# Second attention four heads at a time, another issue order of the last expert weights, and operands at one place modulo 256 bytes

## The chip, the core and the metric

The kernel runs on one core of one Trainium2 chip. The metric is the device time in microseconds; of the kernel before three runs were timed, with a median of 1975.59 us (1973.17 to 1978.7).

## The reference

Two transformer blocks follow each other on 512 tokens of 1024 features, all in float32. What matters of them here:

```python
# block 1
n = rms_norm(h, g_mix); q, k, v, u, bg, cg, ga, gc = split(n @ w_in + b_in)
m = sigmoid(ga) * (chunked_rel_attention(q, k, v) @ w_pa) + sigmoid(gc) * (short_conv(u, bg, cg) @ w_pc)
h = h + m @ w_o
h = h + hier_moe(rms_norm(h, g_ffn))     # 32 experts of width 512, the 2 best of one group for each token
h = h + sigmoid(rms_norm(h, g_ple) @ w_ple_gate + b_ple_gate) * (p @ w_ple_proj)
# block 2: hs = 16 meta tokens and h, 528 rows
for layer in range(2):
    x = rms_norm(hs, norm_mix_pre[layer])
    mix = pool_mixer(x) if layer == 0 else sliding_window_attention(x, k_blk, v_blk)
    hs = hs + rms_norm(mix, norm_mix_post[layer])
    x = rms_norm(hs, norm_ffn_pre[layer])                   # swiglu of width 2816
    hs = hs + rms_norm((silu(x @ w_gate) * (x @ w_up)) @ w_down, norm_ffn_post[layer])
    if layer == 0: k, v = rms_norm(hs, kv_norm) @ w_k + b_k, ... @ w_v + b_v      # 2 heads of 64
# sliding_window_attention: 16 heads of 64, a block of 128 queries sees 128 keys before it and its own 128
logits = q k^T / 8 + bias;  m = max(logits, sink);  p = exp(logits - m);  out = (p / (sum p + exp(sink - m))) v
```

## The kernel before, in words

Block 1 is written out by hand in class `Net`; block 2 is class `Rest`, where generators for "sides" (norms, attention heads, combination) are stepped between the matmuls of a main line, by a planner's clock. In block 2 all instructions are issued through one helper, so that in the profile nearly all of them carry line 1195.

*Matmuls in three terms.* Weights come by DMA as fp32 (`raw`), ScalarE rounds them to fp32r (`whi`) and VectorE takes the rest (`wlo`). A product is `hi*hi + hi*lo + lo*hi` (`mm3`, lines 226 and 1431): three matmuls on TensorE of 128 rows by 256 to 512 columns. The activations are split in the same way: `nT`, `mT`, `pT` in block 1, `x` (normed features, two tiles of 8 x 528) and `act` (four chunks of 528 in each of two tiles, by `act4`, line 1485) in block 2. Layer 0 works on 528 rows, as halves of 256 and 272 columns, layer 1 on 512.

*The second attention* (layer 1) is a side, `heads(t, hq, d)` (line 2018): one block of 128 queries, and of four neighbouring heads the two of one parity `d`. Heads of parity `d` have their queries and keys in partitions 64d to 64d + 63. So the two score matmuls of a call (fp32, 64 rows deep, 256 keys, 144 in the first block, into one PSUM bank) use one half of the array's rows. Maximum and bias on VectorE, exponential on ScalarE and division on VectorE follow, then four transposes into `tmp`, one or two copies to `pt`, two value matmuls (`acc<-pt,v`, 128 rows, two heads side by side as 256 columns, into partitions 0 to 63 of a bank), and `cut` into `oT`. 32 calls are made, in the order of `self.quads` (run, line 2141), up to four in flight: `room("s", 4)` waits for a score buffer. Beside them the main line works on `q`, `kv` and `o_proj`. fp32 matmuls leave two records in the trace, fp32r ones and transposes one.

*The experts* (`moe`, line 834) take weights in half units of 1 MB from a ring of places: `todo` lists them in the order in which they are used, `ring` gives each its place, `load()` issues DMAs on SyncE's queue as long as the next place is free, and a `Take` frees a place once the matmuls on it are issued. `PLACES` is the cycle of 16, `LAST_PLACES` the last eight. `embed_load` (line 621), called two experts before the end, asks for `p`, `w_ple_proj` and `h`; before the last expert `embed_weight` and `embed_turn` split and transpose these, and `embed` (line 648) computes `p @ w_ple_proj` after it. `Rest.run` then starts: `combine` reads the experts' results `y2` back, `bands` and `col` load constants.

*Places.* A tile's place in a partition is the sum of the tiles ahead of it in its pool. By these sums the weights, `wide` and `nT` begin at 64 modulo 256 bytes, `mT` and `pT` at 96, `act` at 224, and rows of 528 fp32 (2112 bytes) move by 64 bytes modulo 256 with every row.

Of the kernel before, what the change touches and what calls it, by code (L numbers as in the profile page):

```python
# [20 lines left out]
P = 128  # L21
D = 1024
S = 512
# [18 lines left out]
LAST_PLACES = ("wide",) * 4 + ("wide2",) * 2 + ("wide",) * 2  # L42
# [91 lines left out]
class Net:  # L134
# [35 lines left out]
    def tmp(self, name="tmp"):  # L170
        self.n_ += 1
        return self.ps.tile([P, 512], F32, tag="tmp", bufs=2, name=f"{name}{self.n_}")

# [91 lines left out]
    def mixer(self):  # L265
# [98 lines left out]
        for t, ps in enumerate(vs):  # L364
            nc.vector.tensor_tensor(vt[:, t], ps, bb[:, 2], OP.add)

# [184 lines left out]
    def head(self):  # L551
# [18 lines left out]
        self.wrt = self.rt.tile([P, KC, 36], F32, name="wr")  # L570
        nc.sync.dma_start(self.wrt[:, :, 0:4], a["w_group"].rearrange("(p kc) n -> p kc n", kc=KC))
# [262 lines left out]
    def moe(self):  # L834
# [145 lines left out]
        with tc.manual_schedule():  # L980
            for e in range(TURN, N_E):
# [252 lines left out]

class Stream:
# [120 lines left out]
class Rest:  # L1356
# [5 lines left out]
    def __init__(self, net, out):  # L1362
# [8 lines left out]
        self.st = Stream(net, self.nc, self.clock)  # L1371
        self.halves = [slice(0, 256), slice(256, L2)]
# [112 lines left out]
    def act4(self):  # L1485

        return [x.rearrange("p (a b) -> p a b", a=4) for x in self.act()]
# [8 lines left out]
    def gain(self, src):  # L1496
        g, was = self.tile("gain", 3, [P, D]), self.clock.cur
        self.nc.sync.dma_start(g, bcast(src, P))
        self.clock.cur = was
        return g  # L1500

    def col(self, src, name):

        g, was = self.one([P, KC], name), self.clock.cur
        self.nc.sync.dma_start(g, src.rearrange("(c p) -> p c", p=P), allow_slow_non_contiguous=True)
# [176 lines left out]
    def pool_weights(self):  # L1682

        a = self.a
        g = self.col(a["norm_mix_pre"][0], "gpool")
# [119 lines left out]
    def up_out(self, pss, A, cs, n, key):  # L1805
# [10 lines left out]
        yield from self.cut(A[0][:, cs], A[1][:, cs], sl)  # L1816
# [201 lines left out]
    def heads(self, t, hq, d):  # L2018
# [6 lines left out]
        hs = slice(4 * hq + d, 4 * hq + 4, 2)  # L2025
# [3 lines left out]
        yield from self.room("s", 4)  # L2029
        place = self.claim("s", 4).append  # L2030
        s = self.scores[self.n_heads % 4]
        self.n_heads += 1
        st = self.net.small.tile([P, 4, 2], F32, tag="st", name="st")
        yield from self.room("acc", 6)
        ps, end = self.acc()
        pv = ps.rearrange("p (a b) -> p a b", a=2)[:, :, :n]
        q, c0, b0 = self.qT[t // 2], P * (t % 2), 64 * d
        e = N_META + (t + 1) * P
        for i in range(2):
            nc.tensor.matmul(pv[:, i], q[b0:b0 + 64, 2 * hq + i, c0:c0 + P], self.kT[g][b0:b0 + 64, e - n:e],  # L2040
                             start=True, stop=True)
        self.mark(("s", t, hq, d))
        yield
        for i in range(2):
            V.tensor_tensor_reduce(s[:, i, :n], pv[:, i], self.bias[hq][:, 2 * i + d, m0:], 1.0, NEG, OP.add, OP.max,
                                   st[:, 0, i:i + 1])
        end(True)
        V.tensor_tensor(st[:, 0], st[:, 0], self.snk[:, hs], OP.max)
        V.tensor_scalar(st[:, 1], st[:, 0], -1.0, None, op0=OP.mult)
        V.tensor_tensor(st[:, 3], self.snk[:, hs], st[:, 0], OP.subtract)  # L2050
        yield
        for i in range(2):
            nc.scalar.activation(s[:, i, :n], s[:, i, :n], AF.Exp, bias=st[:, 1, i:i + 1],
                                 accum_out=st[:, 2, i:i + 1])
# [4 lines left out]
        for i in range(2):  # L2059
            V.tensor_scalar(s[:, i, :n], s[:, i, :n], st[:, 2, i:i + 1], None, op0=OP.mult)  # L2060
        yield
        yield from self.room("pt", 2)
        turn = self.claim("pt", 2).append
        PT = self.tile("pt", 2, [P, 512])
        yield from self.room("tmp", 2)
        ps, end = self.tmp()
        for c, a, b in ((0, 0, k0), (256, k0, n)):
            for i in range(2):
                nc.tensor.transpose(ps[:b - a, c + i * P:c + i * P + P], s[:, i, a:b], self.net.ident)
# [3 lines left out]
        if k0 < P:  # L2073
            nc.scalar.copy(PT[:k0, :256], ps[:k0, :256])
            nc.scalar.copy(PT[:, 256:], ps[:, 256:])
        else:
            nc.scalar.copy(PT, ps)
        end(True)
        yield
        yield from self.room("acc", 6)  # L2080
        ps, end = self.acc()
        vp = self.vt[NT] if t == 0 else self.vt[t - 1]
        gs = slice(64 * g, 64 * g + 64)
        po = ps[0:64, :256]
# [251 lines left out]
```

## Time and profile before

| | before |
|---|---|
| median of 3 runs | 1975.59 us |
| the profiled execution | 1978.86 us |
| its span, first to last instruction | 1977.0 us |
| PE busy | 1928.8 us (98%) |
| DVE busy | 831.9 us (42%) |
| ACT busy | 671.9 us (34%) |
| mean granted clock of PE | 0.986 |

PE is TensorE's matmul queue, PEld its weight loads, DVE VectorE, ACT ScalarE, POOL GpSimd, SP SyncE, which issues the DMAs. Busy time is the union of an engine's instructions; the end of a matmul is modelled, so a busy PE need not be at its peak. `acc<-kt,y 64*128 64x256` is a matmul into tile `acc` with `kt` streamed and `y` stationary: 64 rows by 128 columns of the array, 256 columns streamed. In a timeline neighbours of one kind stand in one row with their count.

### The profile page before, as it was taken

The numbers are of one execution on the slowest core, as the hardware profiler recorded it, in microseconds if no ns is written. First come the engines' busy times: TensorE is split into PE (matmuls) and PEld (weight loads), VectorE is DVE, ScalarE is ACT, GpSimd is POOL, SyncE is SP. The second block draws the span as 40 slices with busy tenths as digits, with TensorE's granted clock in tenths as the row PEclk, the third lists the DMA queues.
The fourth block names the chain that finished last, engine by engine and source line by source line (L and its number), as shares of the span: only waits on it lengthen the run. The fifth ranks groups of instructions, "written<-read, shape, count | busy, mean of one in ns | idle before, by whom it ended". The sixth has DMA issues, their size and how long they took to land. (4 is left out here: it accounts for less than half of the span.)

```text
span 1977.0 us, 27975 instructions
## 1 busy us (share of the span) xinstructions
PE 1928.8 (98%) x11330; PEld 1488.8 (75%) x11330; DVE 831.9 (42%) x1836; ACT 671.9 (34%) x1434; POOL 108.6 (5%) x183
## 2 busy tenths in 40 slices
PE   9999999999999999979999999999999999999998
PEld 7766888754554544527899999999987698888886
DVE  5477343511111111117574333334887874233334
ACT  4333332221111111125463333223876663233232
POOL 2100000010000000001111000000100000000000
PEclk9999999999999999988899999999999999999999
DMA  6222326689999999986035223224432244223322
GB/s 193 79 86 64 106 79 255 229 325 417 417 418 417 418 418 418 405 316 211 2 119 191 86 86 98 74 86 128 140 96 86 86 155 154 85 96 101 102 75 75
DMA packets 182102, 365.59 MB, mean 185 GB/s; under 512 B 25909, under 2 KB 127925, under 8 KB 162514
## 3 DMA queue, kind: packets, MB, share of 16 engines
q1 hardware_dynamic: 178834, 357.47, 49.3%
q0 software_dynamic: 2560, 4.20, 0.6%
q8 instruction: 90, 1.47, 0.3%
q10 hardware_dynamic: 576, 2.10, 0.3%
q14 instruction: 42, 0.34, 0.1%
HBM read 355.34 MB, written 12.58 MB: 186 GB/s over the span
## 5 line engine op out<-in xcount | busy, mean ns | idle before, releaser
L1195 PE MATMUL acc<-x,whi 128*128 128x256 f32 (+2 forms) x2560 | 547.4, 310 | 2.0 <-DVE x L1195 2.0
L1195 PEld LDWEIGHTS acc<-x,whi 128*128 128x128 f32 x2560 | 416.3, 189 | 32.4 <-issue 4.1
L1195 PE MATMUL acc<-x,wlo 128*128 128x256 f32 (+2 forms) x1280 | 395.7, 309 | 0.0
L1195 DVE TENSOR_TENSOR wlo<-raw,whi 128x512 fp32r<-128x512 f32 (+1 forms) x348 | 225.0, 689 | 317.9 <-ACT whi L1195 316.7
L1195 ACT ACTIVATE whi<-raw 128x512 fp32r<-128x512 f32 (+1 forms) x348 | 196.9, 617 | 338.4 <-PE acc L1195 278.9
L1195 PEld LDWEIGHTS acc<-x,wlo 128*128 128x128 f32 x1280 | 241.8, 189 | 12.5 <-DVE wlo L1195 0.2
L104 DVE TENSOR_TENSOR hd<-acc,sl 64x512 f32<-64x512 f32 x32 | 33.9, 1060 | 334.5 <-ACT sl L101 334.5
L1195 PE MATMUL acc<-whi,act 128*128 128x512 f32 x480 | 156.9, 398 | 0.0
L71 PEld LDWEIGHTS tmp<-one,n 128*128 128x128 f32 x1024 | 116.7, 192 | 25.2 <-issue 25.1
L1195 PE MATMUL acc<-act,whi 128*128 128x256 f32 (+1 forms) x704 | 130.5, 286 | 0.6 <-ACT act L1195 0.5
L96 PE MATMUL acc<-wide,xT 128*64 128x512 f32 x544 | 125.2, 603 | 0.0
L71 PE MATMUL tmp<-one,n 128*128 128x128 f32 x1024 | 122.5, 278 | 1.5 <-DVE one L61 1.5
L228 PE MATMUL acc<-wide,whi 128*128 128x512 f32 x288 | 115.5, 401 | 0.0
L230 PE MATMUL acc<-wide,wlo 128*128 128x512 f32 x288 | 112.5, 390 | 0.0
L229 PE MATMUL acc<-wide,whi 128*128 128x512 f32 x288 | 112.2, 390 | 0.0
L1195 PEld LDWEIGHTS acc<-act,whi 128*128 128x128 f32 x704 | 109.3, 188 | 1.1 <-ACT act L1195 0.7
L224 DVE TENSOR_TENSOR wlo<-raw,whi 128x1024 fp32r<-128x1024 f32 x56 | 68.1, 1222 | 96.4 <-ACT whi L221 96.2
L1195 PEld LDWEIGHTS acc<-whi,act 128*128 128x128 f32 x480 | 90.1, 188 | 24.3 <-issue 2.5
L1195 PE MATMUL acc<-act,wlo 128*128 128x256 f32 (+1 forms) x352 | 100.1, 284 | 0.0
L125 ACT COPY ys<-acc 128x512 f32<-128x512 f32 x32 | 18.8, 587 | 224.4 <-PE acc L119 224.4
L1195 PE MATMUL acc<-wlo,act 128*128 128x512 f32 x240 | 95.0, 396 | 0.0
L96 PEld LDWEIGHTS acc<-wide,xT 128*64 128x64 f32 x544 | 37.4, 138 | 67.5 <-issue 66.0
(449 smaller groups left out, 2671.8 us busy)
## 6 DMA issues: line engine op xcount, KB each, us to landing
wide<-in_w_dram SPq DMA_DIRECT2D x92, 1024.0 KB, 15.7
ew<-in_w_dram SPq DMA_DIRECT2D x60, 1024.0 KB, 19.9
raw<-in_w_gate_up_dram SPq DMA_DIRECT2D x52, 1024.0 KB, 5.1
raw<-in_w_in_dram SPq DMA_DIRECT2D x20, 1024.0 KB, 5.2
raw<-in_w_down_dram SPq DMA_DIRECT2D x18, 1024.0 KB, 5.2
raw<-in_w_o_dram SPq DMA_DIRECT2D x12, 1024.0 KB, 5.9
raw<-in_w_q_dram SPq DMA_DIRECT2D x8, 1024.0 KB, 7.0
raw<-in_w_down_dram SPq DMA_DIRECT2D x8, 768.0 KB, 4.5
```

Source lines behind the costliest of these rows:

```text
L71: self.nc.tensor.matmul(self.ps[:, k % 4], self.net.n2[t][:, k * P:(k + 1) * P], self.one[:, t].rearrange("p j s -> p (j s)"), start=t == ...
L96: self.nc.tensor.matmul(self.ps[SL * i:SL * i + SL], x, w(r), start=kc == 0, stop=kc == KC - 1)
L104: self.nc.vector.tensor_tensor(self.hd[SL:].rearrange("q fc p -> q p fc"), v(self.ps[SL:]), v(sl[SL:]), OP.mult)
L125: self.nc.scalar.copy(self.ys, self.py)
L224: self.nc.vector.tensor_tensor(lo, x, hi.bitcast(F32), OP.subtract)
L228: mm(out, l[0], r[0], start=start, stop=False)
L229: mm(out, l[0], r[1], start=False, stop=False)
L230: mm(out, l[1], r[0], start=False, stop=stop)
L1195: r = f(*a, **k)
```

## The change

- *Heads.* `heads(t, hq)` now handles four heads. Its four score matmuls go to two banks, alternating: `d = 0` in the upper and `d = 1` in the lower 64 rows of the array. Bias, maximum, exponential and division stay as many instructions per head; the small operations on `st` cover four heads. Each half of the keys has its own transposes (four into one `tmp`), one copy of 128 x 512 to a `pt` tile, and two value matmuls, where `d` chooses partitions 0 to 63 or 64 to 127 of one bank. One `cut` of all 128 partitions writes `oT`. Two calls are in flight at most; a call needs both `pt` buffers.
- *Last expert weights.* `LAST_PLACES` names two `wide2`, two `y` and four `wide`. `embed_turn` and `embed_weight` come after the last expert.
- *Small loads.* The six columns of gains and bias (`cols`) are loaded in the first block's mixer; `bands` and `combine` change places.
- *Places.* Unused tiles named `even` and the move of `lt` shift `mT` and `pT` by 32 bytes. `Halves` keeps a half of 256 columns in rows of 256 fp32, and the other half behind them: `x` in layer 0 (offset 48 fp32) and in layer 1's first steps up to `o_proj`, and `act` in layer 0. From `o_proj` on layer 1 has `x`, `act` and `oT` in rows of 512. `meta` and `vt` share a tile.

```diff
-LAST_PLACES = ("wide",) * 4 + ("wide2",) * 2 + ("wide",) * 2
+LAST_PLACES = ("wide2",) * 2 + ("y",) * 2 + ("wide",) * 4
...
+        self.cols = {nm: self.col(src, nm) for nm, src in (
+            ("gpool", a["norm_mix_pre"][0]), ("gf0", a["norm_ffn_pre"][0]), ("gkv", a["kv_norm"]),
+            ("gq", a["norm_mix_pre"][1]), ("gf1", a["norm_ffn_pre"][1]), ("bq", a["b_q"]))}
+        self.const.tile([P, 16], F32, name="even")
...
+        self.rt.tile([P, 56], F32, name="even")
...
-        lt = self.lt = self.small.tile([36, P], F32, tag="lt", bufs=1, name="lt")
+        lt = self.lt = self.rt.tile([36, P], F32, tag="lt", bufs=1, name="lt")
...
-                if e == N_E - 1:
-                    self.wproj = [self.embed_weight(hf) for hf in range(2)]
-                    self.embed_turn()
                 expert(e)
+            self.embed_turn()
+            self.wproj = [self.embed_weight(hf) for hf in range(2)]
...
+class Halves:
+
+
+    def __init__(self, t, rows, at=0):
+
+        n = rows * 256
+        self.parts = [x.rearrange("p (a b) -> p a b", a=rows) for x in (t[:, at:at + n], t[:, n:])]
+        self.parts[1] = self.parts[1][:, :, at:at + L2 - 256]
+
+    def __getitem__(self, at):
+        p, k, cs = at
+        c0 = cs.start or 0
+        x = self.parts[c0 >= 256]
+        if c0 >= 256:
+            cs = slice(c0 - 256, cs.stop - 256)
+        assert cs.stop <= x.shape[2]
+        return x[p, k, cs]
+
+
+class Row:
+
+
+    def __init__(self, x, k):
+        self.x, self.k = x, k
+
+    def __getitem__(self, at):
+        return self.x[at[0], self.k, at[1]]
...
-    def room(self, tag, bufs):
+    def room(self, tag, bufs, n=1):
 
         ring = self.rings.setdefault(tag, deque())
-        while len(ring) == bufs and not ring[0]:
+        while not all(list(ring)[:max(0, len(ring) + n - bufs)]):
...
-    def act4(self):
-
-        return [x.rearrange("p (a b) -> p a b", a=4) for x in self.act()]
+    def act4(self, halves=False):
+
+        if halves:
+            return [Halves(x, 4) for x in self.act()]
+        return [x[:, :4 * S].rearrange("p (a b) -> p a b", a=4) for x in self.act()]
...
-                new = self.act4()
+                new = self.act4(halves=not self.wide)
                 for k in range(4):
-                    act[f + k] = [x[:, k] for x in new]
+                    act[f + k] = [Row(x, k) for x in new]
...
-        self.vt = [self.one([P, P], f"v{t}") for t in range(NT + 1)]
-        self.bq = self.col(a["b_q"], "bq")
...
-    def heads(self, t, hq, d):
+    def heads(self, t, hq):
         nc, V = self.nc, self.V
         m0 = P - N_META if t == 0 else 0
         n = 256 - m0
         k0 = n - P
         g = hq // 2
+        snk = self.snk[:, 4 * hq:4 * hq + 4].rearrange("p (i d) -> p d i", d=2)
         yield ("q", t // 2, hq)
         yield ("v", t)
         yield ("v", t - 1 if t else NT)
+        yield from self.room("s", 2)
+        place = self.claim("s", 2).append
+        s = self.scores[self.n_heads % 2]
         self.n_heads += 1
+        st = self.net.small.tile([P, 4, 2, 2], F32, tag="st", name="st", bufs=2)
+        yield from self.room("acc", 6, 2)
+        banks = [self.acc() for _ in range(2)]
+        pv = [ps.rearrange("p (a b) -> p a b", a=2)[:, :, :n] for ps, _ in banks]
+        q, c0 = self.qT[t // 2], P * (t % 2)
+        e = N_META + (t + 1) * P
+        for i in range(2):
+            for d in range(2):
+                b = slice(64 * d, 64 * d + 64)
+                nc.tensor.matmul(pv[d][:, i], q[b, 2 * hq + i, c0:c0 + P], self.kT[g][b, e - n:e], start=True, stop=True)
+        self.mark(("s", t, hq))
+        yield
+        for d in range(2):
+            for i in range(2):
+                V.tensor_tensor_reduce(s[:, d, i, :n], pv[d][:, i], self.bias[hq][:, 2 * i + d, m0:], 1.0, NEG,
+                                       OP.add, OP.max, st[:, 0, d, i:i + 1])
+            banks[d][1](True)
+        V.tensor_tensor(st[:, 0], st[:, 0], snk, OP.max)
+        V.tensor_scalar(st[:, 1], st[:, 0], -1.0, None, op0=OP.mult)
+        V.tensor_tensor(st[:, 3], snk, st[:, 0], OP.subtract)
+        yield
+        for d in range(2):
+            for i in range(2):
+                nc.scalar.activation(s[:, d, i, :n], s[:, d, i, :n], AF.Exp, bias=st[:, 1, d, i:i + 1],
+                                     accum_out=st[:, 2, d, i:i + 1])
+        nc.scalar.activation(st[:, 3], st[:, 3], AF.Exp)
+        yield
+        V.tensor_tensor(st[:, 2], st[:, 2], st[:, 3], OP.add)
+        V.reciprocal(st[:, 2], st[:, 2])
+        for d in range(2):
+            for i in range(2):
+                V.tensor_scalar(s[:, d, i, :n], s[:, d, i, :n], st[:, 2, d, i:i + 1], None, op0=OP.mult)
+        yield
+        PT = []
+        for a, b in ((0, k0), (k0, n)):
+            yield from self.room("pt", 2)
+            turn = self.claim("pt", 2).append
+            x = self.tile("pt", 2, [P, 512])
+            yield from self.room("tmp", 2)
+            ps, end = self.tmp()
+            for d in range(2):
+                for i in range(2):
+                    c = (2 * d + i) * P
+                    nc.tensor.transpose(ps[:b - a, c:c + P], s[:, d, i, a:b], self.net.ident)
+            yield
+            nc.scalar.copy(x[:b - a], ps[:b - a])
+            end(True)
+            PT.append((x[:b - a], turn))
+        place(True)
+        self.next_heads()
+        yield
         yield from self.room("acc", 6)
         ps, end = self.acc()
+        gs = slice(64 * g, 64 * g + 64)
+        v = [(self.vt[NT] if t == 0 else self.vt[t - 1])[:k0, gs], self.vt[t][:, gs]]
+        for j in range(2):
+            for d in range(2):
+                nc.tensor.matmul(ps[64 * d:64 * d + 64, :256], v[j], PT[j][0][:, 256 * d:256 * d + 256],
+                                 start=j == 0, stop=j == 1)
+            PT[j][1](True)
+        yield
+        c = 2 * (hq % 2)
+        o = [x[:, c:c + 2, t * P:(t + 1) * P] for x in self.oT[hq // 2]]
+        yield from self.cut(*o, ps[:, :256].rearrange("p (a b) -> p a b", a=2))
         end(True)
+        self.mark(("a", t, hq))
...
-                self.until(*[("a", t, i, d) for i in range(4) for d in range(2)])
+                self.until(*[("a", t, i) for i in range(4)])
                 if mix is None:
-                    self.until(*[("s", t, i, d) for t in ts for i in range(4) for d in range(2)])
+                    self.until(*[("s", t, i) for t in ts for i in range(4)])
...
-        self.x = [self.one([P, KC, L2], f"x{i}", F32R) for i in range(2)]
-        meta = self.one([N_META, D], "meta")
+        xs = [self.one([P, KC * (256 + 320)], f"x{i}", F32R) for i in range(2)]
+        self.x, self.wide = [Halves(x, KC, 48) for x in xs], False
+        meta = self.tile("meta", 1, [P, D])[:N_META]
...
+        self.side(self.combine(y2))
+        self.step_side()
         self.bands()
         self.rg = self.one([P, NT], "rg")
-        self.side(self.combine(y2))
-        self.step_side()
         self.bg = self.gain(a["b_ple_gate"])
         self.side(self.pool_weights(), 4.0)
         nc.sync.dma_start(meta, a["meta"])
-        self.gkv, self.gq = self.col(a["kv_norm"], "gkvc"), self.col(a["norm_mix_pre"][1], "gqc")
-        self.gf0, self.gf1 = [self.col(a["norm_ffn_pre"][i], f"gf{i}") for i in range(2)]
...
-        self.scores = [x[:, i] for x in [self.big().rearrange("p (a k b) -> p a k b", a=2, k=2) for _ in range(2)]
-                       for i in range(2)]
+        self.scores = [self.big().rearrange("p (a k b) -> p a k b", a=2, k=2) for _ in range(2)]
         self.n_heads = 0
-        self.quads = deque((t, hq, d) for t in (3, 2, 0, 1) for hq in range(4) for d in range(2))
+        self.quads = deque((t, hq) for t in (3, 2, 0, 1) for hq in range(4))
...
+        vt = self.tile("meta", 1, [P, D])
+        self.vt = [vt[:, P * t:P * t + P] for t in range(NT + 1)]
...
-        for _ in range(4):
+        for _ in range(2):
...
+        self.x, self.wide = [x[:, :KC * S].rearrange("p (a b) -> p a b", a=KC) for x in xs], True
...
```

## Rows read from the trace of the kernel before

**Rows 1.** the page: span; busy us (share), instructions of each engine

```profile
span 1977.0 us, 27975 instructions
...
PE 1928.8 (98%) x11330; PEld 1488.8 (75%) x11330; DVE 831.9 (42%) x1836; ACT 671.9 (34%) x1434; POOL 108.6 (5%) x183
```

**Rows 2.** windows, attention: us; busy (x) PE PEld DVE ACT POOL; PEclk, DMA, GB/s

```profile
1425.00:1577.00 152.00, 151.74 (x912) 112.67 (x911) 125.31 (x504) 107.69 (x336) 2.20 (x4) 1.00 0.28 92
```

**Rows 3.** PE timeline, attention: start us, us, operation, shapes, records

```profile
1487.98 0.28 PE L1195 MATMUL acc<-x,wlo 128*128 128x256 f32 x1
1488.19 1.13 PE L1195 MATMUL acc<-kt,y 64*128 64x256 f32 x4
1489.25 1.08 PE L1195 MATMUL acc<-pt,v 128*64 128x256 f32 x4
1490.26 0.51 PE L1195 MATMUL acc<-x,whi 128*128 128x256 f32 x2
1490.60 0.28 PE L1195 MATMUL acc<-x,wlo 128*128 128x256 f32 x1
...
1493.81 0.77 PE L1195 MATMUL acc<-kt,y 64*128 64x144 f32 x8
...
1532.88 1.22 PE L1195 MATMUL acc<-pt,v 16*64 16x256 f32 x4
...
1555.86 1.14 PE L1195 MATMUL acc<-kt,y 64*128 64x256 f32 x8
1556.99 2.09 PE L1195 MATMUL acc<-pt,v 128*64 128x256 f32 x8
```

**Rows 4.** PE timeline, end of experts; in brackets idle time before and releaser

```profile
853.63 3.60 PE L119 MATMUL acc<-wide,hT 128*64 128x512 f32 x16
860.56 1.06 PE L644 MATMUL acc<-ident,n 128*128 128x128 f32 x8 [3.33 <-DMA n<-in_p_dram]
...
868.66 0.46 PE L110 MATMUL acc<-ident,hd 64*128 64x64 f32 x4 [1.76 <-DVE hd L104]
876.62 6.57 PE L119 MATMUL acc<-wide,hT 128*64 128x512 f32 x16 [7.49 <-DMA wide<-in_w_dram]
...
883.11 0.50 PE L228 MATMUL acc<-pwhi,pT 128*128 128x512 f32 x1
...
894.41 0.60 PE L1195 MATMUL tmp<-ident,h 128*128 128x128 f32 x4
```

**Rows 5.** SyncE's queue, end of the experts: start us, us, transfer, count

```profile
817.36 28.52 SPq L874 DMA_DIRECT2D wide<-in_w_dram  x12
...
861.83 4.00 SPq L874 DMA_DIRECT2D wide<-in_w_dram  x2
...
886.53 2.18 SPq L1195 DMA_DIRECT2D act<-y  x4
```

**Rows 6.** windows, before the last expert loads

```profile
834.00:844.00 10.00, 10.00 (x64) 5.53 (x65) 1.49 (x2) 0.59 (x1) 0.00 (x0) 1.00 0.69 256
```

**Rows 7.** windows of 3-term matmuls (512, 512, 256 columns); PE timeline, `mT` stationary

```profile
200.00:360.00 160.00, 160.00 (x704) 131.74 (x703) 60.47 (x70) 46.14 (x54) 1.33 (x6) 1.00 0.43 150
1650.00:1960.00 310.00, 310.00 (x1339) 251.03 (x1338) 109.14 (x171) 93.02 (x168) 0.93 (x1) 1.00 0.28 92
1615.40:1646.20 30.80, 30.80 (x262) 30.70 (x261) 16.85 (x36) 14.30 (x33) 0.00 (x0) 1.00 0.64 210
...
362.94 0.40 PE L228 MATMUL acc<-whi,mT 128*128 128x512 f32 x1
...
367.14 0.40 PE L228 MATMUL acc<-whi,mT 128*128 128x512 f32 x1
```

**Rows 8.** groups by form, attention: count, busy us, mean ns, idle before

```profile
L1195 PE MATMUL acc<-pt,v 128*64 128x256 f32 x112 | 29.9, 391 | 0.1
...
L1195 PE MATMUL acc<-kt,y 64*128 64x256 f32 x96 | 20.1, 401 | 0.1
...
L1195 DVE TENSOR_TENSOR act<-acc,act 64x256 fp32r<-64x256 f32 x32 | 13.2, 414 | 1.1 <-ACT act L1195 0.6
```

More of the change, by code (lines that the diff above doesn't have):

```diff
@@ L172, in tmp, with col @@
         return self.ps.tile([P, 512], F32, tag="tmp", bufs=2, name=f"{name}{self.n_}")
+    def col(self, src, name):
+        g = self.const.tile([P, KC], F32, name=name)
+        self.nc.sync.dma_start(g, src.rearrange("(c p) -> p c", p=P), allow_slow_non_contiguous=True)
+        return g
     def load(self, src, shape):
@@ L1371, in __init__ @@
         self.st = Stream(net, self.nc, self.clock)
+        for nm, x in net.cols.items():
+            setattr(self, nm, x)
         self.halves = [slice(0, 256), slice(256, L2)]
@@ L1498, in gain @@
         self.nc.sync.dma_start(g, bcast(src, P))
[L1499 to L1505, printed above, removed]
         self.clock.cur = was
@@ L1815, in up_out @@
         yield
-        yield from self.cut(A[0][:, cs], A[1][:, cs], sl)
+        yield from self.cut(*[x[:, cs] for x in A], sl)
         place.append(True)
@@ L2028, in heads @@
         yield ("v", t - 1 if t else NT)
-        yield from self.room("s", 4)
-        place = self.claim("s", 4).append
-        s = self.scores[self.n_heads % 4]
+        yield from self.room("s", 2)
+        place = self.claim("s", 2).append
+        s = self.scores[self.n_heads % 2]
         self.n_heads += 1
[L2033 to L2036, printed above, removed]
@@ L2042, in heads @@
-        self.mark(("s", t, hq, d))
+            for d in range(2):
+                b = slice(64 * d, 64 * d + 64)
+                nc.tensor.matmul(pv[d][:, i], q[b, 2 * hq + i, c0:c0 + P], self.kT[g][b, e - n:e], start=True, stop=True)
+        self.mark(("s", t, hq))
         yield
[L2044 to L2047, printed above, removed]
@@ L2051, in heads @@
         yield
-        for i in range(2):
-            nc.scalar.activation(s[:, i, :n], s[:, i, :n], AF.Exp, bias=st[:, 1, i:i + 1],
-                                 accum_out=st[:, 2, i:i + 1])
+        for d in range(2):
+            for i in range(2):
+                nc.scalar.activation(s[:, d, i, :n], s[:, d, i, :n], AF.Exp, bias=st[:, 1, d, i:i + 1],
+                                     accum_out=st[:, 2, d, i:i + 1])
         nc.scalar.activation(st[:, 3], st[:, 3], AF.Exp)
@@ L2058, in heads @@
         V.reciprocal(st[:, 2], st[:, 2])
-        for i in range(2):
-            V.tensor_scalar(s[:, i, :n], s[:, i, :n], st[:, 2, i:i + 1], None, op0=OP.mult)
+        for d in range(2):
+            for i in range(2):
+                V.tensor_scalar(s[:, d, i, :n], s[:, d, i, :n], st[:, 2, d, i:i + 1], None, op0=OP.mult)
         yield
[L2062 to L2069, printed above, removed]
+        PT = []
[13 more added lines that the diff above has]
+            PT.append((x[:b - a], turn))
         place(True)
@@ L2072, in heads @@
         yield
[L2073 to L2079, printed above, removed]
         yield from self.room("acc", 6)
         ps, end = self.acc()
-        vp = self.vt[NT] if t == 0 else self.vt[t - 1]
         gs = slice(64 * g, 64 * g + 64)
-        po = ps[0:64, :256]
-        nc.tensor.matmul(po, vp[:k0, gs], PT[:k0, :256], start=True, stop=False)
-        nc.tensor.matmul(po, self.vt[t][:, gs], PT[:, 256:], start=False, stop=True)
-        turn(True)
+        v = [(self.vt[NT] if t == 0 else self.vt[t - 1])[:k0, gs], self.vt[t][:, gs]]
[4 more added lines that the diff above has]
+            PT[j][1](True)
         yield
         c = 2 * (hq % 2)
-        o = [x[b0:b0 + 64, c:c + 2, t * P:(t + 1) * P] for x in self.oT[hq // 2]]
-        yield from self.cut(*o, po.rearrange("p (a b) -> p a b", a=2))
+        o = [x[:, c:c + 2, t * P:(t + 1) * P] for x in self.oT[hq // 2]]
+        yield from self.cut(*o, ps[:, :256].rearrange("p (a b) -> p a b", a=2))
         end(True)
-        self.mark(("a", t, hq, d))
+        self.mark(("a", t, hq))
     def next_heads(self):
```

8 lines of the change are left out of this document (1 added, 7 removed).

## The prediction

> **What bounds the kernel now.** I read the page first: TensorE (PE) is busy for 1928.8 of 1977.0 us [rows 1], so a stage gets shorter by what its PE queue gets shorter, as long as nothing else is then late. "Busy" here is a union of modelled durations that overlap, so I price matmuls by the distance from one start to the next. Three places matter, each read in another view.
>
> *The second attention (1425 to 1577 us).* PE is busy 151.74 of 152 us, VectorE (DVE) 125.31, ScalarE (ACT) 107.69 [rows 2]. In the order of PE's work a score group of one head pair (four records: two fp32 matmuls, two records each) starts at 1488.19 and the next thing at 1489.25, 1.06 us; a value group takes 1.01 us, to 1490.26 [rows 3]. Where two head pairs of opposite `d` happened to lie side by side, eight score records took 1.13 us from start to start (1555.86 to 1556.99) [rows 3], 1.07 in the median of the five such groups: two row halves of the array worked at once. I went through all groups of the stage in this way: score groups, 22 with 22.6 us from start to start, of which the paired ones already do what the change asks for; value groups, 25 with 32.6 us, none of them concurrent (eight records last 2.09 us, twice four) [rows 3]. The grouped view has the largest forms of both with 20.1 and 29.9 us [rows 8].
>
> *The end of the experts.* PE waits 3.33 us for `p`, 7.49 us for the last expert's down weights, and its 16 last expert matmuls then take 6.57 us against 3.60 for a set that waits for nothing [rows 4]. In SyncE's queue twelve loads fill 817.36 to 845.88; `p`, `w_ple_proj`, `h` and two raw weights were issued behind them, and the two last expert weights behind them at 861.83 [rows 5]. The DMA engines were not full before that: share 0.69 between 834 and 844 [rows 6], because six places were filled from 817.36 and the next load waited for the first of them to be read.
>
> *The spacing of the 3-term matmuls.* With 512 columns it is 160.4 us / 704 = 227.8 ns between 200 and 360 us (weights and `nT`), 310.4/1339 = 231.8 ns in the last feed-forward, and (367.14 - 362.94)/18 = 233.3 ns where `mT` is stationary; 256 columns take 31.1/262 = 118.6 ns [rows 7] (a window counts a matmul that began before it too, so one matmul's 0.4 or 0.3 us is added to its length). Shape and instruction are the same in the first three; what differs is the place of the operands, added up from the tile sizes in the code: `nT` and the weights begin at the same place modulo 256 bytes, `mT` 32 bytes further, and the rows of `x` and `act` (528 fp32, 2112 bytes) move by 64 bytes with every row.
>
> **The change, part by part.** The sum is made against the profiled execution, 1978.86 us (span 1977.0 and 1.9 around it), which lies 3.3 us above the median of the three runs, 1975.59.
>
> *A. Four heads at a time.* Scores: 16 quads instead of 32 pairs. Twelve with 256 keys at the paired 1.07 us, four with 144 at 0.70 (0.77 long, less what overlaps) [rows 3]: 15.6 us, against 22.6: -7.0. Values: the two `d` become column halves of one bank. The trace has no such case in this stage, so I take it from the experts, where column halves alternate: 16 records of 512 columns in 3.60 us [rows 4], 0.22 us each, where a lone record of 256 columns here costs 0.25 and one of 512 would cost about 0.45. So eight records of a quad cost what four cost now: 12 x 1.01 + 4 x 1.15 (the 16-row case, 1.22 long) [rows 3] = 16.7, against 32.6: -15.9. If columns did not run together the term is 0; that is its other bound. Each group also costs its neighbours: the matmul ahead takes 0.21 instead of 0.12 us (1487.98 to 1488.19), and two behind 0.34 instead of 0.24 (1490.26 to 1490.60) [rows 3], 0.2 us a group. 47 groups become 32: -2.9. On PE -25.8 in all. DVE loses 16 cuts of 414 ns [rows 8] and half of its small operations on `st`, some 14 us, and ACT as many cuts. What is late next is DVE: 125 - 14 = 111 of the remaining 126 us, 88% against 82% now, in strict order, with weight splitting behind it on the same queue. So I give back 4 us of stalls: **-22**, bounds -27 (no stall) and -8 (values don't run together and stalls remain).
>
> *B. Last expert weights.* The last eight loads go to `wide2`, `y` and then `wide`, so their places were read 10 to 18 loads earlier and not 6: the queue stays full through 834 to 844 (about 3 us of lost DMA) and the down weights of the last expert are issued ahead of `p`, `w_ple_proj`, `h` and raw (5.5 MB). Expert 31 then runs without `p` in front: 860.56 becomes 857.2, its second half ends at 860.7, DVE's `hd` costs the 1.76 us seen at 868.66, the 16 down matmuls take 3.60 and end near 867.3, not 883.11 [rows 4]. Now the cover is gone for what was moved behind: eight transposes (1.06 us), two cuts of `pT`, two splits of `w_ple_proj` on ACT and DVE. PE waits for these about 3 to 4 us, and embedding, 11.3 us (883.11 to 894.41), ends near 882 to 883.5. The combination needs `y` (four loads, at 886.53 in the kernel before [rows 5]); its scatter starts 15 us earlier but shares full DMA queues, so `y` comes about 12 us earlier, as the embedding does. **-11**, bounds -14 and -5. Six small column loads move from the tail into the first mixer, where they pass the loads of convolution weights and bias on SyncE's queue; both have over 20 us before they are read there, and I cost it at 0 (bounds -2, +2). `bands` and the reordered `combine` are behind the same 4 MB: 0.
>
> *C. Places modulo 256.* Padding moves `mT` and `pT`, and `act`, `oT` and layer 1's `x` lie in rows of 512 or 256 fp32, at the weights' place. 512 columns: 1392 of the last feed-forward and 192 of the output projection by 231.8 - 227.8 = 4.0 ns: -6.3; 240 of `mT` and `pT` by 233.3 - 227.8 = 5.5: -1.3. 912 with 256 columns (layer 1's first four blocks, layer 0's first half of down): between 0 and 118.6 - 113.9 (half of 227.8) = 4.7, taken as 3: -2.7. Together **-10.3**, bounds -14 and -5. Layer 0's `x` (2112 matmuls of up, 480 of k, v and q) gets one constant distance, but by the code 64 bytes before the weights' place. No row shows that distance: an equal place gains, 32 bytes constant lose 1.5 ns of 231.8. Bounds for 2592 matmuls are -4.7 ns (as if equal) and +4 ns (the loss of `mT`, 1.5 ns on each of the two halves of 512 columns, and as much again): -12 and +10 us. A constant distance is nearer to the equal place than to a rotating one in that nothing changes from row to row, so I take half the gain, **-6**. The second half of layer 0's down keeps a rotating row and stays.
>
> Against C stands the Trainium skill, "TensorE: Matmul & The Clock Gate", section Part 2: the engine has two independent SBUF read ports, so loading the next weights takes no read bandwidth from the running matmul. By it the place of an operand would be of no consequence and C would be 0. This case's rows 7 speak against it: 227.8 and 233.3 ns for one instruction and one shape.
>
> Sum: 1978.9 - 22 - 11 - 10.3 - 6 = 1929.6; less 3.3 for the median, **1926 us**.
>
> **The rivals.** (1) *Places don't matter.* The stretches differ in what is streamed beside them too; then C is 0: 1926 + 16 = 1942 us. Against: the fast stretch has more beside it, not less (DVE 60.5 of 160 us and DMA 0.43, against 109.1 of 310 and 0.28 in the slow one) [rows 7]. Chance 0.08. (2) *ACT and DVE bind the attention* and A shrinks to -8: 1940. For it: 88% on DVE in order. Against: PE had 0.3 us idle in the stage, and the quads take work off both. Chance 0.12. The Trainium skill, "TensorEngine Tiling (Array Packing)", section PSUM Bottleneck, warns of this: tiling speeds TensorE, not the emptying of PSUM. The trace agrees in so far as DVE is next. (3) *Layer 0's constant distance is a bad one*: +4 ns each, +10 instead of -6: 1942. Chance 0.10. (4) *Slower than before: latency of the quads.* Only two quads are in flight where four pairs were, and each needs both `pt` buffers. The 32 pairs, four at a time, took 151 us, eight rounds of 18.9. Eight rounds of two quads may last 15.6 us each before PE waits; a quad's own durations add up to about 12 us. B and C take off 27 us elsewhere, so the kernel is slower once a round exceeds (151 + 27)/8 = 22.2 us; at 25 it is 1975.6 + 8 x 2.8 = 1998. Against: the own durations are half of that, and queues on DVE and ACT would have to double them. Chance 0.04. (5) *The column halves don't run together* in this shape: A is -8, as in (2): 1940, chance 0.06.
>
> **How the numbers follow.** Forecast 0.60, rivals 0.08, 0.12, 0.10, 0.04 and 0.06. The bounds of A, B and C together would reach from 1907 (-27, -14, -14, -12 and -2) to about 1970; the upper ends are unlikely to fall together, so the range is 1907 to 1946, which takes in rivals 1, 2, 3 and 5 one at a time and leaves out two of them together and rival 4. About 0.3% (6 us) is what a measurement of this kernel can tell from no change. Faster by more: 0.94; within: 0.02; slower: 0.04.
>
> **What would show it.** A: score and value groups of eight records lasting about 1.1 us each, 16 of each; stage 1425 to 1577 shorter by 20 us or more with DVE near 88%. B: no PE wait for `p` or for the last `wide` loads, embedding about 12 us earlier, DMA share near 1 over 834 to 844. C: spacing near 227 ns for 512 columns throughout the last feed-forward; 113 to 118 in layer 0. The prediction is wrong if PE shows new waits on DVE, ACT or DMA of more than 20 us in all, or if layer 0 gets slower per matmul.

## The result

The changed kernel takes 1945.71 us (median of four runs, 1943.15 to 1947.02), the kernel before 1974.38 in the same session: a ratio of 0.985, 95% interval 0.983 to 0.987. That is 28.7 us less, where 49.6 were forecast (1975.59 to 1926): the time lies at the upper end of the range. The profiled execution took 1945.09 us.

The page after, as [rows 1]: span, and busy us of each engine.

```profile
span 1943.3 us, 27812 instructions
...
PE 1890.7 (97%) x11322; PEld 1473.8 (76%) x11322; DVE 813.4 (42%) x1740; ACT 662.9 (34%) x1394; POOL 107.1 (6%) x183
```

PE lost 38.1 us of busy time, the span 33.7: 4.4 us of idle time came with the change. The attention, as [rows 2] but up to the first matmul of the feed-forward, and in it the stretch between the two parts of the output projection (us; busy PE, PEld, DVE, ACT, POOL; clock, DMA, GB/s):

```profile
1409.97:1570.06 160.09, 149.51 (x999) 119.15 (x999) 123.60 (x443) 113.80 (x333) 3.15 (x7) 0.97 0.31 102
1519.80:1544.60 24.80, 15.97 (x89) 11.52 (x88) 20.50 (x69) 15.04 (x44) 2.05 (x5) 0.79 0.24 86
```

The same stage before, in two windows:

```profile
1425.43:1576.10 150.67, 150.41 (x903) 111.78 (x902) 124.61 (x502) 106.89 (x334) 2.20 (x4) 1.00 0.27 90
1576.10:1597.02 20.92, 20.92 (x107) 17.12 (x105) 16.80 (x39) 15.32 (x39) 1.36 (x3) 1.00 0.40 134
```

The stage took 171.6 us before (1425.43 to 1597.02) and takes 160.1 now: 11.5 less. PE, idle for 0.3 us of it before, is now idle for 10.6, and 8.8 of these lie in the 24.8 us of the second row. TensorE's timeline, as [rows 3]:

```profile
1457.20 1.08 PE L1206 MATMUL acc<-pt,meta 128*64 128x256 f32 x8
1458.21 1.14 PE L1206 MATMUL acc<-kt,y 64*128 64x256 f32 x8
1459.28 0.66 PE L1206 MATMUL tmp<-ident,big 128*128 128x128 f32 x4
...
1519.83 0.39 PE L1206 MATMUL acc<-whi,act 128*128 128x512 f32 x1
1520.22 1.46 PE L1206 MATMUL tmp<-ident,big 128*128 128x128 f32 x8
1527.89 1.97 PE L1206 MATMUL acc<-pt,meta 128*64 128x256 f32 x8 [6.21 <-ACT pt L1206]
1529.79 2.08 PE L1206 MATMUL acc<-kt,y 64*128 64x256 f32 x8
...
1536.20 3.68 PE L1206 MATMUL tmp<-dg,h 128*128 128x128 f32 x16 [1.90 <-ACT pt L1206]
...
1540.83 1.14 PE L1206 MATMUL acc<-kt,y 64*128 64x256 f32 x8
...
1544.63 0.48 PE L1206 MATMUL acc<-whi,act 128*128 128x512 f32 x1
```

A value group and a score group of a quad last 1.08 and 1.14 us (1.01 and 1.07 from start to start), as forecast. Then, from 1519.83 to 1544.63, PE has nothing but the last quads and the norms: it waits 6.21 us for `pt`, and the groups behind that run at half the clock (2.08 us for scores; the granted clock is 0.50, 1.2 of 2.4 GHz, from 1527.90 to 1531.80). `pt` is the copy of the transposed probabilities out of `tmp`, which ScalarE makes. Its queue in that wait holds a norm that waits for VectorE, four weight roundings, then the two copies:

```profile
1524.57 0.63 ACT L1206 ACTIVATE junk<-y 128x512 bf16<-128x512 f32 x1 [2.33 <-DVE y L1206]
...
1525.19 2.17 ACT L1206 ACTIVATE whi<-raw 128x512 fp32r<-128x512 f32 x4
1527.27 1.05 ACT L1206 COPY pt<-tmp 128x512 f32<-128x512 f32 x2
```

The end of the experts, as [rows 4] (PE), [rows 5] (SyncE's queue) and [rows 6] (window):

```profile
862.14 3.65 PE L119 MATMUL acc<-wide,hT 128*64 128x512 f32 x16 [0.56 <-issue]
865.73 1.09 PE L656 MATMUL acc<-ident,n 128*128 128x128 f32 x8
868.50 0.50 PE L234 MATMUL acc<-pwhi,pT 128*128 128x512 f32 x1 [1.68 <-ACT pwhi L227]
869.76 0.50 PE L235 MATMUL acc<-pwlo,pT 128*128 128x512 f32 x1 [0.76 <-DVE pwlo L230]
...
872.61 0.63 PE L234 MATMUL acc<-pwhi,pT 128*128 128x512 f32 x1
...
882.20 0.60 PE L1206 MATMUL tmp<-ident,h 128*128 128x128 f32 x4
```

```profile
838.87 3.78 SPq L886 DMA_DIRECT2D wide<-in_w_dram  x4
842.94 0.39 SPq L638 DMA_DIRECT2D n<-in_p_dram  x1
...
872.38 2.65 SPq L1206 DMA_DIRECT2D act<-y  x4
```

```profile
834.00:844.00 10.00, 10.00 (x54) 4.07 (x55) 0.43 (x1) 1.17 (x2) 0.82 (x1) 1.00 1.01 419
```

DMA is full from 834 on, neither `p` nor a weight is waited for, and the next operation after the embedding starts 12.2 us earlier than before (882.20 against 894.41) [rows 4].

### The profile page after: what moved, and what is told of

It is laid out like the page before. It is cut to its first block, busy times and chain, and to the rows that moved or that the text cites. A ratio compares the mean times of both kernels' runs of the same rounds, so it can differ in the third digit from the quotient of the medians.

```text
span 1943.3 us, 27812 instructions
## 1 busy us (share of the span) xinstructions
PE 1890.7 (97%) x11322; PEld 1473.8 (76%) x11322; DVE 813.4 (42%) x1740; ACT 662.9 (34%) x1394; POOL 107.1 (6%) x183
## 4 chain that ended last, share of the span: by engine, by line
PE 49%; issue 21%; DVE 3%; ACT 2%; POOL 2%; DMA 1%; POOLq 0%; DVEq 0%; ACTq 0%; another core or an unknown queue 0%; SPq 0%
PE acc L1206 46%; PE tmp L1206 3%; POOL y L128 1%; DVE wlo L1206 1%; DVE h L1206 1%; ACT whi L1206 1%; DMA act<-y 0%; DVE big L1206 0%; DMA raw<-in_w_q_dram 0%; ACT junk L1206 0%; ACT big L1206 0%; DMA y<-ys,si 0%; DVE x L1206 0%; DVE y L1206 0%; ACT kt L1206 0%
## 5 line engine op out<-in xcount | busy, mean ns | idle before, releaser
L1206 PE MATMUL acc<-x,whi 128*128 128x256 f32 (+2 forms) x2560 | 539.2, 308 | 0.1
L1206 PE MATMUL acc<-whi,act 128*128 128x512 f32 x480 | 152.0, 392 | 0.0
L71 PEld LDWEIGHTS tmp<-one,n 128*128 128x128 f32 x1024 | 116.7, 192 | 25.2 <-issue 25.1
```

The costliest lines, as they stand in the source:

```text
L71: self.nc.tensor.matmul(self.ps[:, k % 4], self.net.n2[t][:, k * P:(k + 1) * P], self.one[:, t].rearrange("p j s -> p (j s)"), start=t == ...
L1206: r = f(*a, **k)
```

## The experiments

The kernel before, timed beside these runs, had medians from 1974.38 to 1977.25 us, so a difference of 2 us between two versions shows nothing.

**One part undone at a time.** `no_four` has `heads(t, hq, d)`, four score buffers and 32 pairs in place of

```diff
-    def heads(self, t, hq):
...
-        self.quads = deque((t, hq) for t in (3, 2, 0, 1) for hq in range(4))
```

> The changed kernel with the old attention: two heads at a time, four pairs in flight. Theory 1 (the gain of the quads was eaten by stalls of TensorE near the end of the attention, and the rest of the change is independent of it): from the first score to the first feed-forward matmul after it the two traces differ by 171.6 - 160.1 = 11.5 us, so this is slower than the changed kernel (1945.7 us) by 10 to 12, about 1957 us. Theory 2 (the quads bring the 22 us of my prediction and something else lost 10 us): about 1968 us.

1957.02 us (1956.33 to 1957.46), 11.3 above the changed kernel: theory 1. Its attention:

```profile
1411.64:1582.44 170.80, 170.21 (x1007) 128.26 (x1007) 141.27 (x539) 121.91 (x373) 3.61 (x7) 1.00 0.29 95
```

PE is as full as before, 170.2 of 170.8 us. Against the changed kernel the quads take off 20.7 us of busy time, and 10.0 of these come back as idle time.

`no_order`:

```diff
-LAST_PLACES = ("wide2",) * 2 + ("y",) * 2 + ("wide",) * 4
+LAST_PLACES = ("wide",) * 4 + ("wide2",) * 2 + ("wide",) * 2
...
+                if e == N_E - 1:
+                    self.wproj = [self.embed_weight(hf) for hf in range(2)]
+                    self.embed_turn()
                 expert(e)
-            self.embed_turn()
-            self.wproj = [self.embed_weight(hf) for hf in range(2)]
```

> The changed kernel with the old places of the last eight expert weights and with embed_turn and embed_weight ahead of the last expert. Theory 1: the two traces differ by 15.2 us until the last expert's matmul and by -2.4 - 3.3 + 0.5 us in the embedding, 10.0 in all; so about 1956 us, with the waits of 3.3 us for p and 7.5 us for the last down weights back. Theory 2 (what matters here is when y comes back, and the small column loads that were moved give the gain): under 1950 us.

1952.67 us (1951.93 to 1954.44): 7.0 above the changed kernel. Neither number was met; the waits did come back:

```profile
858.68 1.94 PE L656 MATMUL acc<-ident,n 128*128 128x128 f32 x8 [3.31 <-DMA n<-in_p_dram]
...
875.38 5.00 PE L119 MATMUL acc<-wide,hT 128*64 128x512 f32 x16 [7.02 <-DMA wide<-in_w_dram]
```

`no_places`:

```diff
-        self.rt.tile([P, 56], F32, name="even")
...
-        return [x[:, :4 * S].rearrange("p (a b) -> p a b", a=4) for x in self.act()]
+        return [x.rearrange("p (a b) -> p a b", a=4) for x in self.act()]
...
-        xs = [self.one([P, KC * (256 + 320)], f"x{i}", F32R) for i in range(2)]
-        self.x, self.wide = [Halves(x, KC, 48) for x in xs], False
+        xs = [self.one([P, KC, L2], f"x{i}", F32R) for i in range(2)]
+        self.x, self.wide = xs, True
...
-        self.x, self.wide = [x[:, :KC * S].rearrange("p (a b) -> p a b", a=KC) for x in xs], True
+        self.x, self.wide = xs, True
```

> The changed kernel without the alignment: mT and pT 32 bytes off, x and act in rows of 528 floats that move by 64 bytes from row to row. Theory 1 (the place modulo 256 bytes sets the spacing): the 512-column matmuls with mT, act and x go from 227 to 232 or 233 ns, some 1800 x 5 = 9 us; layer 0's 272 columns from 123.4 to 125.9, 1104 x 2.5 = 2.8 us; 256 columns lie within 1 us; about 1958 us. Rival 1 of the prediction (places don't matter): 1946 us and 227 ns as in the changed kernel.

1955.16 us (1953.13 to 1961.84), 9.5 above the changed kernel, with an interval of the ratio that leaves some 6 us on each side; the two spans differ by 11.9. Places matter, as the spacings below show more sharply than the times: rival 1 of the prediction is out. Together the three parts undone are 27.8 us, the whole is 28.7; by the ratios to the kernel before, each in its own session, they are some 24 of 30.

`no_small` loads the six columns at their old place, and `bands` ahead of `combine`:

```diff
...
+        self.bands()
+        self.rg = self.one([P, NT], "rg")
         self.side(self.combine(y2))
         self.step_side()
-        self.bands()
-        self.rg = self.one([P, NT], "rg")
...
+        self.gkv, self.gq = self.col("gkv"), self.col("gq")
+        self.gf0, self.gf1 = [self.col(f"gf{i}") for i in range(2)]
```

> The changed kernel with the six small columns loaded where they were before, behind the read-back of y and among the weights of the gate, and with bands ahead of combine again. Theory (the small loads were worth what the order of the last weights falls short of the two traces' difference: from the last embedding matmul to layer 0 the kernel before took 99.3 us and the changed kernel with the old order of weights 96.6): 2 to 4 us slower than the changed kernel, 1948 to 1950 us. Rival, my prediction's 0: 1946 us.

1944.63 us (1943.42 to 1947.25): no difference. The prediction's 0 was right and my new theory wrong. The stretch that misled me, from the last embedding matmul to layer 0, takes 95.6 to 100.7 us in the twelve kernels here that have the small loads where the changed one has them (98.7 in that itself): two single traces can't show 2 us in it.

**What stalls the quads.** `three` gives the attention a third score buffer:

```diff
-        g, was = self.tile("gain", 3, [P, D]), self.clock.cur
+        g, was = self.tile("gain", 2, [P, D]), self.clock.cur
...
-        yield from self.room("s", 2)
...
+        yield from self.room("s", 3)
...
+        self.scores.append(self.tile("big3", 1, [P, D]).rearrange("p (a k b) -> p a k b", a=2, k=2))
...
-        for _ in range(2):
+        for _ in range(3):
```

> The changed kernel with a third score buffer, so that three quads are in flight (gains get two buffers instead of three to make room). Theory 1 (the second half of the output projection waits for the last scores, and these wait for a score buffer, because only two quads are in flight): the 24.8 us between the two parts of the output projection on TensorE shrink to about 10, with no wait of 6 us in them, and the whole takes 6 to 10 us less, 1936 to 1940 us. Theory 2 (the wait comes from ScalarE's queue, where six weight roundings and a norm stand ahead of the two pt copies): the same 24.8 us within 3, 1944 to 1948 us.

1938.19 us in a single run: theory 1's number. `copy_now` was to take the other suspect away, the queue in front of the copies:

```diff
-            yield
             nc.scalar.copy(x[:b - a], ps[:b - a])
```

> The changed kernel with the copy of a transposed half to pt issued right behind its transposes, so that no weight rounding and no norm comes between on ScalarE's queue. Theory 2: the wait of 6.2 us for pt is gone, half clock behind it too; 5 to 8 us less, 1938 to 1941 us. Theory 1: the wait moves to another step of the last quads; within 3 us of 1945.7.

1946.96 us in a single run, and PE waits for `pt` as long as before (us in total, times, longest):

```profile
PE acc L1206 <- ACT pt L1206: 7.6, 2, 6.2
```

But the edit did not shorten that queue. In this trace, too, a norm that waits for VectorE and four roundings stand ahead of the copies:

```profile
1523.10 0.63 ACT L1206 ACTIVATE junk<-y 128x512 bf16<-128x512 f32 x1 [1.68 <-DVE y L1206]
...
1523.73 2.17 ACT L1206 ACTIVATE whi<-raw 128x512 fp32r<-128x512 f32 x4
1525.81 1.04 ACT L1206 COPY pt<-tmp 16x512 f32<-16x512 f32 x2
```

So `copy_now` decides nothing between the two theories. What the traces show is this: all ten kernels here with two quads in flight have the wait of 6.2 us, and 22.8 to 27.4 us between the two parts of the output projection; the two runs with three quads have no such wait, and 0.6 us. `act192` below, which like `three` has two buffers for gains, keeps the wait. In the changed kernel the transposes end at 1521.68 and the copies start at 1527.27: at that place PE waits for what stands ahead on ScalarE's queue, and with two quads in flight it has nothing else to do meanwhile. A third quad is enough to end the stall; whether copies ahead of the roundings would do as much with two quads is not shown. The same kernel as `three`, run five times:

> Three quads in flight again, timed. Theory (the stage from the first score to the first feed-forward matmul lost 7.7 us by the third score buffer, 152.4 against 160.1 us, and nothing else changed): 1938 us, 7 to 8 us below the changed kernel's 1945.7. Rival (the one look was a favourable run): 1943 us or more.

1938.65 us (1935.73 to 1942.46), ratio to the kernel before 0.981 (0.979 to 0.982): 7.1 us faster than the changed kernel (8.5 by the two ratios), the best version here.

```profile
1412.86:1565.29 152.43, 146.93 (x1000) 115.34 (x999) 123.39 (x443) 112.17 (x335) 4.22 (x7) 1.00 0.33 109
```

```profile
1523.20 1.14 PE L1206 MATMUL acc<-kt,y 64*128 64x256 f32 x8
...
1532.53 0.39 PE L1206 MATMUL acc<-whi,act 128*128 128x512 f32 x1
1532.76 0.60 PE L1206 MATMUL tmp<-ident,big 128*128 128x128 f32 x4
1533.11 0.47 PE L1206 MATMUL acc<-whi,act 128*128 128x512 f32 x1
```

The last scores are at 1523.20 instead of 1540.83, and the second part of the output projection, which may not start before them (`until(("s", t, i))` in `o_proj`), follows the first without a pause (1533.11). Against `no_four` the stage is 18.4 us shorter (170.8 - 152.4) and PE busy for 23.3 less.

**What places are worth.** `table` gives the eight rows of `x` every distance to the weights in multiples of 32 bytes, and the four rows of `act` the first four of them:

```diff
...
-        self.x, self.wide = [x[:, :KC * S].rearrange("p (a b) -> p a b", a=KC) for x in xs], True
+        self.x, self.wide = [x[:, :KC * 520].rearrange("p (a b) -> p a b", a=KC) for x in xs], True
```

> The changed kernel with the rows of x 32 bytes further from row to row in layer 1 (512 columns) and in layer 0's first half (256 columns), 96 bytes in its second half (272 columns), so that every multiple of 32 bytes occurs as distance between x and the weights; act in layer 1 likewise 0 to 96 bytes. One look at the spacing by distance. Theory 1 (equal places are best at 512 columns, and only there): 227 ns at distance 0 and 231 to 234 at all others; at 256 columns distance 0 is the worst with 120 ns and 192 bytes give 116. Theory 2 (what counts is that the distance doesn't change from row to row): 512 columns give 227 ns at every distance within a row and more only at the change of rows.

1956.85 us, and both theories fell: with rows that move no row of `x` has 227 ns at 512 columns, not even the one at distance 0 (231.4 in the mean of its three matmuls; the others 231.1 to 234.3). So `const_a`, `const_b` and `const_c` hold one distance over a whole stage; two of the edits of `const_a` (it moves `mT`, `pT` and layer 0's `x` in the same way):

```diff
...
-        return [x[:, :4 * S].rearrange("p (a b) -> p a b", a=4) for x in self.act()]
+        return [x[:, 16:16 + 4 * S].rearrange("p (a b) -> p a b", a=4) for x in self.act()]
...
-        self.x, self.wide = [x[:, :KC * S].rearrange("p (a b) -> p a b", a=KC) for x in xs], True
+        self.x, self.wide = [x[:, 32:32 + KC * S].rearrange("p (a b) -> p a b", a=KC) for x in xs], True
```

> The changed kernel with other constant distances to the weights: x of layer 1 at 128 bytes (864 matmuls of 512 columns), act of layer 1 at 64 (720), mT and pT at 64, x of layer 0 at 0 (256 and 272 columns). Theory 1 (an equal place is needed at 512 columns): x, act and mT go from 227 to 231-234 ns, some 1776 x 5 = 9 us; layer 0's x at 0 goes from 116.9 and 123.4 to 119 to 120 and 125 to 126, 2600 x 2.5 = 5 us at most; about 1957 us. Theory 2 (a distance that stays constant over the whole stage is enough): 227 ns at 128 and 64 too, only mT's 32 bytes of before being bad; 1946 to 1950 us.

> As const_a with x of layer 1 at 192 bytes, act of layer 1 and mT and pT at 128, x of layer 0 at 96. Theory 1: 512 columns at 231 to 234 ns, layer 0 between its values at 0 and at 192; about 1957 us. Theory 2: 227 ns and 1946 to 1950 us.

> As const_a and const_b with x of layer 1 at 32 bytes, act of layer 1 and mT and pT at 192, x of layer 0 at 160. Theory (at 512 columns an equal place alone gives 227 ns): 231 to 234 ns for all of them; layer 0's x between 117 and 120 ns at 256 columns, 123.4 and 125.4 at 272; about 1957 us. Rival (several distances are as good): 227 to 229 ns at 32 or 192.

1957.80, 1958.46 and 1954.32 us, a single run each. Windows of the last feed-forward: 80 us in which `x` streams, then 42 in which `act` is stationary (changed kernel, `no_places`, `const_a`, `const_b`, `const_c`). The second number is PE's busy time, and the count in brackets behind it its matmuls: the more, the closer they follow each other.

```profile
1710.00:1790.00 80.00, 80.00 (x355) 66.24 (x354) 27.89 (x44) 25.12 (x44) 0.00 (x0) 1.00 0.32 106
1795.00:1837.00 42.00, 42.00 (x187) 34.79 (x186) 16.08 (x25) 9.41 (x17) 0.00 (x0) 1.00 0.25 80
```

```profile
1715.00:1795.00 80.00, 80.00 (x347) 64.86 (x346) 27.91 (x44) 24.52 (x44) 0.00 (x0) 1.00 0.29 93
1803.00:1845.00 42.00, 42.00 (x183) 34.01 (x182) 15.44 (x24) 10.06 (x18) 0.00 (x0) 1.00 0.23 76
```

```profile
1715.00:1795.00 80.00, 80.00 (x345) 64.83 (x345) 27.74 (x44) 24.01 (x43) 0.00 (x0) 1.00 0.29 93
1803.00:1845.00 42.00, 42.00 (x182) 33.84 (x181) 15.45 (x24) 9.81 (x18) 0.00 (x0) 1.00 0.23 76
```

```profile
1715.00:1795.00 80.00, 80.00 (x345) 64.45 (x344) 27.76 (x43) 24.17 (x44) 0.00 (x0) 1.00 0.28 92
1804.00:1846.00 42.00, 42.00 (x183) 34.04 (x182) 15.65 (x24) 9.76 (x18) 0.00 (x0) 1.00 0.23 76
```

```profile
1712.00:1792.00 80.00, 80.00 (x345) 64.37 (x344) 27.78 (x43) 24.15 (x44) 0.00 (x0) 1.00 0.28 92
1801.00:1843.00 42.00, 42.00 (x185) 34.53 (x184) 15.76 (x24) 9.88 (x18) 0.00 (x0) 1.00 0.23 76
```

From start to start over whole stretches, in ns:

| distance in bytes | 0 | 32 | 64 | 96 | 128 | 160 | 192 | rows moving by 64 |
|---|---|---|---|---|---|---|---|---|
| 512 columns, `x` streams | 226.7 | 233.3 | | | 232.7 | | 233.3 | 231.7 |
| 512 columns, `act` or `mT` stationary | 227.0 | 233.2 | 233.3 | | 232.4 to 232.7 | | 229.0 | 231.9 |
| 256 columns, `x` streams (layer 0) | 119.7 | | | 119.8 | | 117.5 | 116.7 to 117.3 | 117.7 |
| 272 columns, `x` streams (layer 0) | 125.4 | | | 125.4 | | 123.5 | 123.4 | 126.0 |

With 512 columns a constant distance isn't enough, the place has to be equal. With 256 and 272 columns it is the other way round: 192 and 160 bytes are best, and an equal place is worse than moving rows at 256 columns (119.7 and 117.7) and little better at 272 (125.4 and 126.0). `act192` tries this on another operand, `act` of layer 0:

```diff
-        return [self.tile(f"act{i}", 2, [P, 4 * L2], F32R) for i in range(2)]
+        return [self.tile(f"act{i}", 2, [P, 4 * 576], F32R) for i in range(2)]
...
-            return [Halves(x, 4) for x in self.act()]
+            return [Halves(x, 4, 48) for x in self.act()]
...
-        g, was = self.tile("gain", 3, [P, D]), self.clock.cur
+        g, was = self.tile("gain", 2, [P, D]), self.clock.cur
```

> The changed kernel with act of layer 0 at 192 bytes from the weights in both halves (rows of 256 and 320 floats; gains get two buffers to make room). Theory (for 256 and 272 columns 192 bytes is the best distance, whatever streams): the 528 down matmuls with 256 columns go from 119.7 to about 117 ns, those with 272 from 126 to about 123.4 ns; 2.9 us less. Rival (x has another reason, its rows are long in use): 119 to 120 and 126 ns as in the changed kernel.

117.2 and 123.4 ns from start to start where the changed kernel has 119.8 (equal place) and 126.1 (rows that move): the theory. Its down matmuls by form (count, busy us, mean ns), and those of the changed kernel:

```profile
L1206 PE MATMUL acc<-act,whi 128*128 128x272 f32 x352 | 66.2, 287 | 0.6 <-ACT act L1206 0.5
L1206 PE MATMUL acc<-act,whi 128*128 128x256 f32 x352 | 63.6, 282 | 0.0
```

```profile
L1206 PE MATMUL acc<-act,whi 128*128 128x272 f32 x352 | 67.6, 290 | 0.6 <-ACT act L1206 0.5
L1206 PE MATMUL acc<-act,whi 128*128 128x256 f32 x352 | 64.9, 284 | 0.0
```

From its first to its last down matmul layer 0 takes 296.9 us instead of 299.2, and 299.2 to 300.7 in six other kernels with the places of the changed one. The time is 1942.94 us in a single run, which is too near to 1945.71 to show a gain. There was no room in SBUF for this and the third score buffer together.

## Why the prediction was right in sign and short in size

- **A, -22: 11.3.** The PE work was foreseen well: with three quads in flight scores take 15.4 us (15.6 forecast) and values 17.4 (16.7), against 22.6 and 32.6 in the pairs of `no_four`, and PE's busy time falls by 23.3 (25.8 forecast with the neighbours). The step that failed is the stall: 4 us were given back; 10.6 idle us came, and 2.6 at half clock (busy time 149.5 against 146.9 with the third buffer). I looked for it in DVE's 88%, and DVE was busy for 123.6 of 160.1 us (77%). Late were the copies to `pt`, behind other work on ScalarE's queue, with only two quads in flight. That is rival 4's mechanism, but I had priced it over the whole stage, where the main line's matmuls hide it (a round needs to exceed 15.6 us). It bites only where that cover is gone: between the two parts of the output projection the main line waits for the last scores, they wait for a score buffer, and 24.8 us hold nothing else. Rival 2 had the size (-8), but too much work on DVE and ACT is not what the runs show: with a third quad in flight the same work on DVE and ACT leaves PE 5.5 us idle, not 10.6. Rival 5 is out: the column halves do run together.
- **B, -11: 7.0.** The queue filled, both waits went, and PE waits for `w_ple_proj`'s splits for 1.68 + 0.76 = 2.4 us, near the 3 to 4 forecast. Mis-sized is what follows the first of them: seven of the embedding's matmuls ran at half clock (0.63 us long instead of 0.40; granted clock 0.50 from 870.9 to 873.9), and from first to last it took 13.5 us instead of 11.1, the second wait of 0.76 included. The half clock is not a fixed price of these waits: in `three`, with 1.68 and 0.77 us of them, the granted clock stayed at 1.00 and the embedding took 11.8 us. In the twelve kernels with this order it took 11.8 to 13.6. Against `no_order` it ended 9.1 us earlier (881.97 and 891.09), and not 11 to 12. The other 2 us lie in the stretch up to layer 0, which varies by as much; what they are stays open. Small loads: 0 forecast, none found.
- **C, -10.3 and -6.** With 512 columns 5.0 ns were gained with `x` and `act` (4.0 forecast) and 6.2 with `mT` and `pT` (5.5): 1584 x 5.0 + 240 x 6.2 = 9.4 us against 7.6. The extrapolation to 256 columns failed: -2.7 forecast, and a loss of 0.9 came (119.8 ns for `act` instead of 118.9, and 0.5 us in layer 1's first blocks). Layer 0's `x` gained about 4.1 us of the 6 forecast (1104 x 2.6 with 272 columns and some 1488 x 0.8 with 256): "half the gain" was a guess between bounds, and that it came near was luck, because 192 bytes are a good distance for these shapes, which nothing in the trace of before showed. By spacing 9.4 - 0.9 + 4.1 = 12.6 of 16.3, by undoing the part 9.5 +- 6. One sign of being wrong came in part: layer 0's down got slower per matmul (118.9 to 119.8 ns and 125.6 to 126.1), its up faster.
- The profiled execution of before lay 4.5 us above the median of its four runs, not 3.3.

The Trainium skill, "TensorE: Matmul & The Clock Gate", section Part 2, says that the engine has two independent SBUF read ports and that loading the next weights takes no read bandwidth from the running matmul. It does not speak of places; I read it as C = 0, and the runs speak against that reading: 226.7 and 233.3 ns for one instruction and one shape, by the place of one operand alone. The Trainium skill, "TensorEngine Tiling (Array Packing)", section PSUM Bottleneck, warns that tiling speeds TensorE but not the evacuation of PSUM. What PE waited 6.21 us for was such a copy, but the engines that make them were not full (DVE busy for 20.5 and ACT for 15.0 of those 24.8 us), and with a third score buffer and the same copies 7.1 us came back.

## What to carry to other kernels

Where four small steps are packed into one, check how many of the larger steps are in flight at the end of the stage, where no independent work hides their latency, and what waits for the last of them: here one more buffer brought back two thirds of what was lost (7.1 of 10.7 us). Measure an alignment for each shape: the place that is best with 512 columns was a bad one with 256. And expect that TensorE may run at half clock behind a wait that a move leaves: it did behind the 6.21 us, and in some of the kernels behind the embedding's 1.68.

## Not expected of the hardware

- The spacing of fp32r matmuls depends on the distance of the two operands by 3%, in opposite ways at 512 columns (226.7 ns at 0, 233.3 at 192 bytes when streamed) and at 256 (119.7 and about 117). That 256 bytes is a period shows in `no_places`, where each row of `x` lies 64 bytes further: the spacing of its eight rows with 512 columns repeats after four (230.1, 232.8, 232.5, 231.8, then 230.0, 232.7, 232.3, 231.6 ns). Why the place matters, and why rows that move never reach 227 ns in the mean of a row, no run here shows.
- Two column halves and two row halves of the array both run together with fp32: eight records of a value group take 1.014 us from start to start, four of a pair 1.008; for scores it is 1.065 and 1.057.
